# A state space output turned from token-major to channel-major, in a one-core hybrid layer kernel

## The chip, the core and the metric

The kernel runs on one core of a Trainium2 chip. The metric is the device time of one launch in microseconds (us). Beside it there is one profiled execution, from which all rows below are read.

## The reference, cut to what matters

Two layers, each a feed-forward block, a mixer and a second feed-forward block, over 256 tokens of width 1024, all in float32. The change touches the state space half of the mixer:

```python
x = xh * dt[..., None]                                  # 16 heads of 64 channels, 256 tokens
decay = segsum_exp(adt)                                 # per head, 256 x 256, causal
cb = einsum('bclgn,bcsgn->bcgls', cc, bc)               # per group (2 groups of 8 heads)
y = einsum('bcgls,bcgels,bcsgep->bclgep', cb, decay, x) # one chunk of 256: no carried state
...
y = y + xh * d_skip[:, None]
y = y.reshape(bsz, L, D_SSD) * silu(z)
yg = y.reshape(bsz, L, SSD_GROUPS, D_SSD // SSD_GROUPS)
yg = yg * rsqrt(mean(yg * yg, axis=-1) + EPS)           # norm over the 512 channels of a group
return yg.reshape(bsz, L, D_SSD) * norm_g
```

The projection `u = rmsnorm(h) @ w_mix_in` gives z, the convolved channels, dt, q, k, v and the index vectors. The mixer ends with one product of the concatenated state space and attention outputs with `w_mix_out`.

## The kernel before

**Products.** Every large product is done with its operands split into a high and a low part (`whi`/`wlo` for weights, pairs of `tT` tiles for activations), three matmuls for each block of 128 rows. Token-major products (function `three`, lines 182 to 184) hold 128 tokens as the stationary operand and stream 512 weight columns. Channel-major products (lines 866 to 868) hold 128 weight columns and stream all 256 tokens. Small products in plain float32 are one call in the code and two passes in the trace.

**Weights.** `Stream` loads blocks of 2048 columns into `raw` (three buffers), ScalarE makes `whi` (line 127), VectorE makes `wlo` (line 128), three blocks ahead of their use. The DMAs are issued on SyncE's queue.

**Order.** `MIX_ORDER` says in which order the mixer's column blocks are projected. A number is a pair of 128-channel chunks for the convolution, a name is a token-major block: `z0` and `z1` are the two halves of the gate z. Side work is written as generators, `index` (choice of keys), `steps` (decay sums), `ssd` (state space) and `attention`. `flow.step` advances one of them between parts of the projection, `flow.defer` puts a function off by a number of units, `flow.unit` is called after each part. The scheduler then orders each engine's instructions; what is given to `keep_in_program_order` stays behind the instruction traced ahead of it on its engine.

**The state space part.** `conv` (lines 671 to 688) makes each 128-channel chunk `chan[c]`, channels on partitions and tokens along the row. `by_token` turns the chunks into `xs`, tokens on partitions. `ssd` makes, for each group g and for four heads at a time, the matrices `m0` (tokens 0 to 127 against all 256) and `m1` (tokens 128 to 255 against themselves): a DMA broadcasts the decay sums (line 717), ScalarE takes differences and exponentials (lines 719 to 724), VectorE multiplies by dt and cb (lines 727, 729). Then come the products of lines 739 and 743: the matrix is the stationary operand (128 x 128), 64 columns of `xs` stream, 24 such calls in a group. `finish_y` adds x times `d_skip` (GpSimd, line 753; VectorE, line 759), multiplies by silu(z) (line 760), sums squares on ScalarE (`square_sum`, line 427), scales by the row's inverse norm (line 767), and in `turn_y` transposes eight blocks on TensorE (line 774) and splits them into `yT` pairs (`split_scaled`, lines 405 and 407). `yT[0]` to `yT[7]` are read by the mixer's `out_product`.

**PSUM.** Four pools of two banks: `mm` and `ac` for products, `sd` for small products, `tp` for transposes. The state space products hold both `ac` banks.

Of the kernel before, what the change touches and what calls it, by code (L numbers as in the profile page):

```python
# [52 lines left out]
def hybrid_kernel(  # L53
# [39 lines left out]
    def ttile():  # L93
        return tT.tile([P, L], FR, name="tT", tag="tT")
# [98 lines left out]
    for name, c0 in (("z", C_Z), ("q", C_Q), ("k", C_K), ("v", C_V)):  # L193
        for n in range(2):
            MIX_COLS[f"{name}{n}"] = [(c0 + 512 * n, 512)]
    MIX_ORDER = ["idx0", "idx1", 8, "z0", 10, 0, "z1", 2, 4, "q0", 6, "q1", "k0", "k1", "v0", "v1"]
# [106 lines left out]
    heads = const.tile([P, 3, DEPTH, H_SSD], F32, name="heads")  # L303
# [21 lines left out]
    def setup():  # L325
# [4 lines left out]
        with tc.tile_pool(name="setup", bufs=1, reuse_waits="tile") as tmp:  # L330
# [13 lines left out]
            for i, v in enumerate((dt_bias, a_log, d_skip)):  # L344
                later(heads[:, i], v.partition_broadcast(P))
            yield
# [193 lines left out]
    def mixer(l, norm, after):  # L540
        with ExitStack() as mctx:
# [25 lines left out]
            sz, xs = (big8().rearrange("p (t c) -> p t c", t=NT) for _ in range(2))  # L567
# [102 lines left out]

            def conv(c, ps):
                xr = ms.tile([P, L + 3], F32, name="xr", bufs=2)
                nc.gpsimd.memset(xr[:, 0:3], 0.0)
                nc.vector.tensor_mul(xr[:, 3:], ps, rb)

                def w(j):
                    o = (l * 4 + j) * 12 + c
                    return convs[:, o:o + 1]
                o = 96 + l * 12 + c
                acc = row1k()  # L680
                nc.scalar.activation(acc, xr[:, 0:L], AF.Identity, scale=w(0), bias=convs[:, o:o + 1])
                for j in range(1, 4):
                    nc.vector.scalar_tensor_tensor(acc, xr[:, j:j + L], w(j), acc, op0=ALU.mult, op1=ALU.add)
                dst = ms.tile([P, L], F32, name="chan" if c < 8 else "bcs", bufs=4)
                nc.scalar.activation(dst, acc, AF.Silu)
                chan[c] = dst
                if c in (3, 7):
                    flow.defer(lambda: by_token(c // 4), 3)
# [10 lines left out]
            def ssd():  # L699
# [9 lines left out]
                for g in range(G_SSD):  # L709
# [23 lines left out]
                    pss = [bank(ac) for _ in range(NT)]  # L733
                    for t in range(NT):
                        ps = pss[t]
                        for h in range(8):
                            o = ps[:, h * 64:(h + 1) * 64]
                            m0, m1 = ms4[h // 4]
                            nc.tensor.matmul(o, m0[:, h % 4, t * P:(t + 1) * P],  # L739
                                             half[:, 0, h * 64:(h + 1) * 64],  # L740
                                             start=True, stop=(t == 0))
                            if t:
                                nc.tensor.matmul(o, m1[:, h % 4], half[:, 1, h * 64:(h + 1) * 64],
                                                 start=False, stop=True)
# [3 lines left out]
            def finish_y(g, half, pss):  # L748

                sq = [None] * NT  # L750
                for t in range(NT):
                    y = half[:, t].rearrange("p (h c) -> p h c", c=HD_SSD)
                    nc.gpsimd.tensor_tensor(y, y, bc(heads[:, 2, l, 8 * g:8 * g + 8], [P, 8, HD_SSD], 2),
                                            ALU.mult)

                def gate():
                    for t in range(NT):
                        y = half[:, t]
                        nc.vector.tensor_add(y, pss[t], y)
                        nc.vector.tensor_mul(y, y, sz[:, t, 512 * g:512 * g + 512])  # L760
                        sq[t] = square_sum(y, "y")
                    flow.defer(scale)

                def scale():
                    for t in range(NT):
                        rg = inv_rms([sq[t]], D_SSD // G_SSD, "y")
                        nc.vector.tensor_scalar(half[:, t], half[:, t], rg, None, op0=ALU.mult)
                    flow.defer(turn_y)

                def turn_y():  # L770
                    for t in range(NT):
                        ps = bank(tp)
                        for i in range(4):
                            nc.tensor.transpose(ps[:, i * P:(i + 1) * P], half[:, t, i * P:(i + 1) * P], ident)
                        ks = range(4 * g, 4 * g + 4)
                        for k in ks:
                            if yT[k] is None:
                                yT[k] = (ttile(), ttile())
                        split_scaled(ps, [(yT[k], gain(3, l, k)) for k in ks], t)

                flow.defer(gate)


# [74 lines left out]
            for what in MIX_ORDER:  # L858
                if isinstance(what, int):
                    hi, lo = stream.take()  # L860
                    for j in range(2):
# [9 lines left out]
                        flow.unit(0)  # L871
                        conv(what + j, ps)
# [5 lines left out]
                for t, ps in project(norm, n, kind not in "qkv"):  # L878
# [9 lines left out]
                    elif kind == "z":  # L888
                        nc.scalar.activation(sz[:, t, 512 * half:512 * half + 512], ps, AF.Silu, scale=r[t])
# [96 lines left out]
```

## Time and profile before

| | |
|---|---|
| three runs | 1214.01, 1214.35, 1215.32 us; median 1214.35 |
| profiled execution | 1215.21 us, of which its span (first to last instruction) is 1213.5 us |
| TensorE busy | 1198.1 us, 99% of the span, in 5997 instructions |
| VectorE busy | 729.4 us, 60% |
| ScalarE busy | 636.6 us, 52% |
| GpSimd busy | 112.8 us, 9% |
| DMA | 214.25 MB, mean 177 GB/s |

A TensorE instruction's duration in the trace holds its way through the array too, so that instructions overlap: what one costs in a row of like ones is the distance from one start to the next.

### The profile page before, as it was taken

How to read it: one execution, taken by the hardware profiler on the slowest of the kernel's cores; microseconds unless marked ns; L12 is line 12 of the kernel's file. 1: busy time of each engine (PE TensorE's matmuls, PEld its weight loads, DVE VectorE, ACT ScalarE, POOL GpSimd, SP SyncE). 2: the span in 40 equal slices, each digit the busy share in tenths (PEclk: the TensorE clock that was granted, in tenths of full speed). 3: DMA queues.
4: the chain of work that ended last, by engine and by line, in shares of the span. 5: the costliest groups of instructions: out<-in, count | busy, mean ns of one | idle time of the engine just before them, and what ended most of it. 6: DMA issues, size and time to landing. Idle time of an engine off the chain costs nothing.

```text
span 1213.5 us, 15334 instructions
## 1 busy us (share of the span) xinstructions
PE 1198.1 (99%) x5997; PEld 1003.0 (83%) x5997; DVE 729.4 (60%) x963; ACT 636.6 (52%) x864; POOL 112.8 (9%) x216
## 2 busy tenths in 40 slices
PE   8999999999999999999999999999999999999997
PEld 6788888988888888888888888898978888888886
DVE  5655545687597565454464554466867965554543
ACT  5544435657776454444354443366578655444432
POOL 0200000602320000000000000015133100000000
PEclk9999999999999999999999999999999999999999
DMA  7665554654533465564646545566454435556550
GB/s 253 204 202 166 190 190 149 225 174 159 188 140 125 152 202 162 192 206 175 201 151 203 188 163 206 164 200 202 156 174 154 163 135 173 185 165 205 188 193 35
DMA packets 149100, 214.25 MB, mean 177 GB/s; under 512 B 8100, under 2 KB 115364, under 8 KB 149028
## 3 DMA queue, kind: packets, MB, share of 16 engines
q1 hardware_dynamic: 147604, 208.52, 51.9%
q0 software_dynamic: 1280, 4.23, 1.0%
q8 instruction: 47, 0.77, 0.3%
q10 hardware_dynamic: 144, 0.52, 0.1%
q14 instruction: 25, 0.20, 0.1%
HBM read 212.17 MB, written 1.08 MB: 176 GB/s over the span
## 4 chain that ended last, share of the span: by engine, by line
PE 93%; DVE 2%; ACT 2%; DMA 1%; POOL 1%; issue 0%; SPq 0%; ACTq 0%; POOLq 0%; DVEq 0%
PE mm L182 15%; PE mm L184 15%; PE mm L183 15%; PE ac L183 12%; PE ac L184 12%; PE ac L182 12%; PE tp L511 2%; PE ac L739 1%; DMA raw<-in_w_ffn_in_dram 1%; PE mm L866 1%; PE ac L868 1%; PE mm L868 1%; PE ac L867 1%; PE mm L867 1%; PE ac L866 1%; PE sd L800 1%
## 5 line engine op out<-in xcount | busy, mean ns | idle before, releaser
L128 DVE TENSOR_TENSOR wlo<-raw,whi 128x2048 fp32r<-128x2048 f32 (+3 forms) x206 | 451.2, 2195 | 337.5 <-ACT whi L127 337.1
L127 ACT CAST whi<-raw 128x2048 fp32r<-128x2048 f32 (+3 forms) x206 | 376.6, 1835 | 295.7 <-PE ac L184 186.7
L182 PE MATMUL mm<-whi,tT 128*128 128x512 f32 (+1 forms) x672 | 267.6, 398 | 0.5 <-ACT s L894 0.5
L184 PE MATMUL mm<-whi,tT 128*128 128x512 f32 (+1 forms) x672 | 260.8, 388 | 0.4 <-DVE tT L407 0.4
L183 PE MATMUL mm<-wlo,tT 128*128 128x512 f32 (+1 forms) x672 | 260.1, 387 | 0.0
L182 PE MATMUL ac<-whi,tT 128*128 128x512 f32 (+1 forms) x480 | 190.0, 396 | 1.0 <-ACT tT L405 0.5
L183 PE MATMUL ac<-wlo,tT 128*128 128x512 f32 (+1 forms) x480 | 185.1, 386 | 0.8 <-DVE wlo L128 0.8
L184 PE MATMUL ac<-whi,tT 128*128 128x512 f32 (+1 forms) x480 | 185.2, 386 | 0.0
L184 PEld LDWEIGHTS mm<-whi,tT 128*128 128x128 f32 x672 | 126.2, 188 | 26.0 <-DVE tT L407 0.9
L182 PEld LDWEIGHTS mm<-whi,tT 128*128 128x128 f32 x672 | 126.3, 188 | 25.1 <-issue 1.3
L183 PEld LDWEIGHTS mm<-wlo,tT 128*128 128x128 f32 x672 | 126.5, 188 | 22.7 <-DVE wlo L128 0.2
L182 PEld LDWEIGHTS ac<-whi,tT 128*128 128x128 f32 x480 | 90.2, 188 | 17.9 <-ACT whi L127 1.2
L183 PEld LDWEIGHTS ac<-wlo,tT 128*128 128x128 f32 x480 | 90.4, 188 | 17.6 <-DVE wlo L128 1.9
L184 PEld LDWEIGHTS ac<-whi,tT 128*128 128x128 f32 x480 | 90.2, 188 | 17.7
L421 POOL TENSOR_TENSOR r_x<-ms_x,mhalf 128x1 f32<-128x1 f32 x14 | 9.7, 695 | 869.3 <-DVE ms_x L419 861.8
L182 PE MATMUL ac<-whi,hT_hi 128*128 128x512 f32 x176 | 69.2, 393 | 0.0
L182 PE MATMUL mm<-whi,hT_hi 128*128 128x512 f32 x176 | 69.0, 392 | 0.0
L184 PE MATMUL ac<-whi,hT_lo 128*128 128x512 f32 x176 | 68.6, 390 | 0.0
L184 PE MATMUL mm<-whi,hT_lo 128*128 128x512 f32 x176 | 68.6, 390 | 0.0
L183 PE MATMUL mm<-wlo,hT_hi 128*128 128x512 f32 x176 | 68.5, 389 | 0.0
L183 PE MATMUL ac<-wlo,hT_hi 128*128 128x512 f32 x176 | 68.5, 389 | 0.0
L533 ACT ACTIVATE s1k<-ac,r_x 128x256 f32<-128x256 f32 x44 | 20.7, 472 | 67.5 <-PE ac L184 64.7
(217 smaller groups left out, 1449.0 us busy)
## 6 DMA issues: line engine op xcount, KB each, us to landing
raw<-in_w_ffn_in_dram SPq DMA_DIRECT2D x172, 512.0 KB, 5.0
raw<-in_w_ffn_out_dram SPq DMA_DIRECT2D x44, 1024.0 KB, 4.8
raw<-in_w_mix_in_dram SPq DMA_DIRECT2D x44, 1024.0 KB, 5.1
raw<-in_w_mix_out_dram SPq DMA_DIRECT2D x16, 1024.0 KB, 4.8
s<-csum POOLq DMA_DIRECT2D x8, 512.0 KB, 4.0
raw<-in_w_mix_in_dram SPq DMA_DIRECT2D x4, 600.0 KB, 3.8
raw<-in_w_mix_in_dram SPq DMA_DIRECT2D x4, 568.0 KB, 3.9
raw<-in_w_ffn_in_dram SPq DMA_DIRECT2D x8, 256.0 KB, 3.2
```

The source lines that it names most:

```text
L127: pin(nc.scalar.copy(hi[:, o], raw[:, o]))
L128: pin(nc.vector.tensor_sub(lo[:, o], raw[:, o], hi[:, o].bitcast(F32)))
L182: nc.tensor.matmul(ps, xh, whi, start=first, stop=False)
L183: nc.tensor.matmul(ps, xh, wlo, start=False, stop=False)
L184: nc.tensor.matmul(ps, xl, whi, start=False, stop=last)
L511: nc.tensor.transpose(ps[:, f * L + t * P:f * L + (t + 1) * P], hs[:, t, f * P:(f + 1) * P], ident)
L533: nc.scalar.activation(sg, ps[:, 0:256], AF.Silu, scale=norm.r[t])
L739: nc.tensor.matmul(o, m0[:, h % 4, t * P:(t + 1) * P], half[:, 0, h * 64:(h + 1) * 64], start=True, stop=(t == 0))
L800: nc.tensor.matmul(ps[:, j * nk:(j + 1) * nk], qT[:, hg + h0 + j, t * P:(t + 1) * P], kT[:, hg + h0 + j, 0:nk], start=True, stop=True)
L866: nc.tensor.matmul(ps, hi[:, o:o + P], xh, start=(k == 0), stop=False)
L867: nc.tensor.matmul(ps, hi[:, o:o + P], xl, start=False, stop=False)
L868: nc.tensor.matmul(ps, lo[:, o:o + P], xh, start=False, stop=(k == KD - 1))
```

## The change

The z chunks are projected channel-major, as the convolution's chunks are (-8, -6, -4, -2 in `MIX_ORDER` stand for them), and `gate` multiplies by the row of inverse norms (VectorE) and takes silu (ScalarE). The state space products swap operands: 64 columns of `xs` are stationary, `m0` and `m1` stream over 256 and 128 tokens, and two heads write partitions 0 to 63 and 64 to 127 of one bank, that is, use two halves of the array's columns. What follows is done with channels on partitions: skip, gate and squares; the sum over channels by a matmul against a column of ones; the inverse norm brought back as a row by a matmul against the identity; the last scaling and the split into `yT`, without transposes. `d_skip` is laid out by channel with two element-wise DMAs.

```diff
-    MIX_ORDER = ["idx0", "idx1", 8, "z0", 10, 0, "z1", 2, 4, "q0", 6, "q1", "k0", "k1", "v0", "v1"]
+    MIX_ORDER = ["idx0", "idx1", 8, -8, -6, 10, 0, -4, -2, 2, 4, "q0", 6, "q1", "k0", "k1", "v0", "v1"]
...
-            for i, v in enumerate((dt_bias, a_log, d_skip)):
+            for i, v in enumerate((dt_bias, a_log)):
                 later(heads[:, i], v.partition_broadcast(P))
+            for i in range(2):
+                later(skips[64 * i:64 * i + 64], d_skip.rearrange("l (c i) -> i l c", i=2)[i].partition_broadcast(64),
+                      allow_slow_non_contiguous=True)
...
+            def gate(c, ps):
+                nc.vector.tensor_mul(sz[:, c], ps, rb)
+                nc.scalar.activation(sz[:, c], sz[:, c], AF.Silu)
...
-                dst = ms.tile([P, L], F32, name="chan" if c < 8 else "bcs", bufs=4)
+                dst = ms.tile([P, L], F32, name="chan" if c < 8 else "bcs", bufs=8 if c < 8 else 4)
...
-                    pss = [bank(ac) for _ in range(NT)]
-                    for t in range(NT):
-                        ps = pss[t]
-                        for h in range(8):
-                            o = ps[:, h * 64:(h + 1) * 64]
-                            m0, m1 = ms4[h // 4]
-                            nc.tensor.matmul(o, m0[:, h % 4, t * P:(t + 1) * P],
-                                             half[:, 0, h * 64:(h + 1) * 64],
-                                             start=True, stop=(t == 0))
-                            if t:
-                                nc.tensor.matmul(o, m1[:, h % 4], half[:, 1, h * 64:(h + 1) * 64],
-                                                 start=False, stop=True)
+                    pss = [bank(ac) for _ in range(2)]
+                    for h in range(0, 8, 2):
+                        o = pss[h // 4][:, h % 4 * P:h % 4 * P + L]
+                        m0, m1 = ms4[h // 4]
+                        for j in range(2):
+                            tc.keep_in_program_order(
+                                nc.tensor.matmul(o[64 * j:64 * j + 64], half[:, 0, (h + j) * 64:(h + j + 1) * 64],
+                                                 m0[:, (h + j) % 4], start=True, stop=False))
+                        for j in range(2):
+                            tc.keep_in_program_order(
+                                nc.tensor.matmul(o[64 * j:64 * j + 64, P:], half[:, 1, (h + j) * 64:(h + j + 1) * 64],
+                                                 m1[:, (h + j) % 4], start=False, stop=True))
...
+                y = half.rearrange("p b (i t) -> p b i t", i=2)
+
+                def gated():
+                    for b in range(2):
+                        z = sz[:, 4 * g + 2 * b:4 * g + 2 * b + 2]
+                        for i in range(2):
+                            c = 4 * g + 2 * b + i
+                            nc.vector.scalar_tensor_tensor(y[:, b, i], chan[c], skips[:, l, c:c + 1],
+                                                           pss[b][:, i * L:(i + 1) * L],
+                                                           op0=ALU.mult, op1=ALU.add)
+                        nc.vector.tensor_mul(y[:, b], y[:, b], z)
+                        nc.scalar.activation(z, y[:, b], AF.Square)
+                    z = sz[:, 4 * g:4 * g + 4]
+                    nc.vector.tensor_add(z[:, 0:2], z[:, 0:2], z[:, 2:4])
+                    nc.vector.tensor_add(z[:, 0], z[:, 0], z[:, 1])
+                    flow.defer(sums, 2)
+
+                def sums():
+                    ps = bank(sd)
                     for t in range(NT):
+                        nc.tensor.matmul(ps[:, t:t + 1], sz[:, 4 * g, t * P:(t + 1) * P], ones[:, 0:1],
+                                         start=True, stop=True)
+                    m, rg = (small.tile([P, NT], F32, name=n) for n in ("ms_y", "r_y"))
+                    nc.vector.tensor_scalar(m, ps[:, 0:NT], 2.0 / D_SSD, EPS, op0=ALU.mult, op1=ALU.add)
+                    nc.gpsimd.tensor_tensor(rg, m, mhalf.to_broadcast([P, NT]), ALU.pow)
+                    flow.defer(lambda: row(rg))
+
+                def row(rg):
+                    rT = bank(sd)[:, :L]
                     for t in range(NT):
+                        nc.tensor.matmul(rT[:, t * P:(t + 1) * P], rg[:, t:t + 1].to_broadcast([P, P]), ident,
+                                         start=True, stop=True)
+                    scale(rT)
+
+                def scale(rT):
+                    for b in range(2):
+                        for i in range(2):
+                            k = 4 * g + 2 * b + i
+                            hi, lo = ttile(), ttile()
+                            nc.vector.scalar_tensor_tensor(y[:, b, i], y[:, b, i], gain(3, l, k), rT,
+                                                           op0=ALU.mult, op1=ALU.mult)
+                            nc.scalar.copy(hi, y[:, b, i])
+                            nc.vector.tensor_sub(lo, y[:, b, i], hi.bitcast(F32))
+                            yT[k] = (hi, lo)
...
-                        flow.unit(0)
-                        conv(what + j, ps)
+                        flow.unit(what < 0)
+                        if what < 0:
+                            gate(8 + what + j, ps)
+                        else:
+                            conv(what + j, ps)
```

The old bodies of `finish_y` (lines 750 to 781) and the silu of the z blocks (line 889) are taken out.

## Rows read from the trace of the kernel before

**Rows 1.** The page: busy time of the engines, and the granted TensorE clock.
```profile
PE 1198.1 (99%) x5997; PEld 1003.0 (83%) x5997; DVE 729.4 (60%) x963; ACT 636.6 (52%) x864; POOL 112.8 (9%) x216
...
PEclk9999999999999999999999999999999999999999
```
**Rows 2.** Windows, TensorE alone: block z0, then chunk pairs 10 and 0.
```profile
220.91:232.41 11.50, 11.50 (x55) 1.00 0.62 215
232.41:243.93 11.52, 11.52 (x98) 1.00 0.64 189
```
**Rows 3.** Groups by line and shape, TensorE.
```profile
L739 PE MATMUL ac<-s,s 128*128 128x64 f32 x128 | 19.3, 271 | 0.0
...
L743 PE MATMUL ac<-s,s 128*128 128x64 f32 x64 | 12.4, 275 | 0.0
...
L774 PE MATMUL tp<-ident,s 128*128 128x128 f32 x32 | 4.6, 276 | 0.7 <-DVE s L767 0.7
```
**Rows 4.** Timeline of TensorE: transposes, a run of state space products, projection again.
```profile
315.69 0.60 PE L845 MATMUL tp<-ident,s 128*128 128x128 f32 x4
316.12 1.23 PE L739 MATMUL ac<-s,s 128*128 128x64 f32 x10
...
318.52 0.39 PE L743 MATMUL ac<-s,s 128*128 128x64 f32 x2
318.72 0.48 PE L182 MATMUL mm<-whi,tT 128*128 128x512 f32 x1
319.03 0.40 PE L183 MATMUL mm<-wlo,tT 128*128 128x512 f32 x1
```
**Rows 5.** Timeline of TensorE: float32 products over 256 and 128 columns.
```profile
293.08 0.59 PE L704 MATMUL sd<-bcs 128*128 128x256 f32 x2
293.51 0.38 PE L705 MATMUL sd<-bcs 128*128 128x128 f32 x2
293.73 0.60 PE L704 MATMUL sd<-bcs 128*128 128x256 f32 x2
```
**Rows 6.** Timeline of TensorE: index products, 64 rows each, on two halves of the rows.
```profile
302.37 0.39 PE L184 MATMUL mm<-whi,tT 128*128 128x512 f32 x1
302.69 1.14 PE L641 MATMUL sd<-s 64*128 64x256 f32 x8
303.76 0.50 PE L182 MATMUL mm<-whi,tT 128*128 128x512 f32 x1
304.09 0.40 PE L183 MATMUL mm<-wlo,tT 128*128 128x512 f32 x1
```
**Rows 7.** Timeline of TensorE: the last run of state space products in layer 0.
```profile
345.07 0.88 PE L739 MATMUL ac<-s,s 128*128 128x64 f32 x6
```
**Rows 8.** Groups by line and shape, VectorE.
```profile
L407 DVE SCALAR_TENSOR_TENSOR tT<-tp,gains,tT 128x128 fp32r<-128x128 f32 x128 | 36.1, 341 | 14.9 <-ACT tT L405 14.9
L683 DVE SCALAR_TENSOR_TENSOR s1k<-xr,convs,s1k 128x256 f32<-128x256 f32 x72 | 34.6, 485 | 5.9 <-ACT s1k L681 5.1
...
L828 DVE TENSOR_TENSOR tT<-sd,tT 128x256 fp32r<-128x256 f32 x16 | 6.4, 420 | 7.0 <-ACT tT L827 7.0
...
L759 DVE TENSOR_TENSOR s<-ac,s 128x512 f32<-128x512 f32 x8 | 5.4, 676 | 3.9 <-POOL s L753 3.9
...
L767 DVE TENSOR_SCALAR s<-s,r_y 128x512 f32<-128x512 f32 x8 | 3.9, 484 | 2.4 <-POOL r_y L421 2.3
```
**Rows 9.** Windows, all engines: z stretch, then the stretch of the state space products.
```profile
220.90:256.00 35.10, 35.10 (x217) 30.84 (x216) 23.00 (x31) 23.53 (x31) 16.54 (x32) 1.00 0.59 191
320.00:370.00 50.00, 49.44 (x273) 41.91 (x272) 42.09 (x91) 38.43 (x78) 12.88 (x23) 1.00 0.41 139
```
**Rows 10.** Waits of SyncE's queue.
```profile
SPq L114 <- DVE wlo L128: 691.7, 109, 10.2
```
**Rows 11.** The page's DMA queue: packets, MB, share of 16 engines.
```profile
q1 hardware_dynamic: 147604, 208.52, 51.9%
```

More of the change, by code (lines that the diff above doesn't have):

```diff
@@ L192, in hybrid_kernel @@
     }
-    for name, c0 in (("z", C_Z), ("q", C_Q), ("k", C_K), ("v", C_V)):
+    for name, c0 in (("q", C_Q), ("k", C_K), ("v", C_V)):
         for n in range(2):
             MIX_COLS[f"{name}{n}"] = [(c0 + 512 * n, 512)]
-    MIX_ORDER = ["idx0", "idx1", 8, "z0", 10, 0, "z1", 2, 4, "q0", 6, "q1", "k0", "k1", "v0", "v1"]
+    MIX_ORDER = ["idx0", "idx1", 8, -8, -6, 10, 0, -4, -2, 2, 4, "q0", 6, "q1", "k0", "k1", "v0", "v1"]
     X_BEFORE = {0: [(0, 0)], 1: [(1, 0)], 2: [], 4: [(0, 1), (1, 1)], 6: []}
@@ L302, in hybrid_kernel @@
     convs = const.tile([P, 120], F32, name="convs")
-    heads = const.tile([P, 3, DEPTH, H_SSD], F32, name="heads")
+    heads = const.tile([P, 2, DEPTH, H_SSD], F32, name="heads")
+    skips = const.tile([P, DEPTH, H_SSD // 2], F32, name="skips")
     a_neg = const.tile([P, DEPTH, H_SSD], F32, name="a_neg")
@@ L566, in mixer @@
             csum = rowsums.tile([H_SSD, L], F32, name="csum", tag="csum")
-            sz, xs = (big8().rearrange("p (t c) -> p t c", t=NT) for _ in range(2))
+            sz = big8().rearrange("p (c t) -> p c t", c=8)
+            xs = big8().rearrange("p (t c) -> p t c", t=NT)
             kT, qT = (big8().rearrange("p (h c) -> p h c", h=H_ATT) for _ in range(2))
@@ L748, in finish_y @@
             def finish_y(g, half, pss):
[L750 to L756, printed above, removed]
-                    for t in range(NT):
[L758 to L762, printed above, removed]
@@ L764, in scale @@
-                def scale():
-                    for t in range(NT):
[L766 to L779, printed above, removed]
@@ L781, in finish_y @@
-                flow.defer(gate)
+                y = half.rearrange("p b (i t) -> p b i t", i=2)
[13 more added lines that the diff above has]
+                    flow.defer(sums, 2)
@@ L784, in attention @@
+                flow.defer(gated)
             def attention():
@@ L887, in mixer @@
                                                        op0=ALU.mult, op1=ALU.add)
-                    elif kind == "z":
-                        nc.scalar.activation(sz[:, t, 512 * half:512 * half + 512], ps, AF.Silu, scale=r[t])
                     elif kind == "v":
```

## The prediction

> **What bounds the kernel now.** Read the page's busy times first: TensorE is busy in 99% of the span and its granted clock reads 9 (90% or more of full speed) in every slice [rows 1], that is, it stays at the 2.4 GHz level. VectorE stands at 60%, ScalarE at 52%. So the time is the sum of TensorE's starts, and a change is worth what it adds to or takes from that sum, unless another engine starts to hold TensorE up. Next the groups by line, for how many passes each small product has [rows 3]; then the timeline around them, because a group's mean duration (0.27 us) holds the way through the array, while the distance between starts is the cost [rows 4 to 6]; last the windows of the two stretches that change, for the room on the other engines [rows 9].
>
> **The change, step by step.**
>
> *z by channel.* Block z0 takes 11.50 us with five index transposes inside [rows 2]. Four transposes take 0.43 us [rows 4], so the five cost 0.54, with some 0.1 for coming back; 10.9 us are left for 48 passes over 512 columns, 0.227 each. Two chunk pairs, the same weights with weights stationary and 256 columns streaming, take 11.52 us [rows 2]: 96 passes, 0.120 each. So each z block costs 0.6 us more, and there are four: **+2.4 us**. VectorE gets 16 multiplications of 128x256 in each layer, 0.42 us each (as line 828's [rows 8]), 6.7 us in each layer of a region where it is busy 23.0 of 35.1 us [rows 9]; ScalarE takes as many silus in place of eight longer ones. Both fit in, so I cost them at nothing. If they didn't, every us that a bank comes free late would stand on TensorE's path. The weights come in pieces of 1 KB in place of 2 KB, as the chunk pairs' do; the DMA share with them is 0.64, with z0 0.62 [rows 2]: nothing.
>
> *The products of the state space part.* Now 192 passes [rows 3]. A run of 24 (10 and seven pairs) goes from 316.12 to 318.72, 0.108 each [rows 4]: 20.8 us. They stream only 64 columns, so something other than the stream sets this pace. Afterwards there are 64 calls, 128 passes, half over 256 columns, half over 128, each on half of the array's columns. In plain float32 a pass over 256 columns costs 0.215 us and one over 128 costs 0.11 [rows 5]. If the halves do not overlap: 64 x 0.215 + 64 x 0.11 = 20.8 us, no gain. If they overlap fully, half: 10.4 us. No row shows two column halves; the nearest are the index products on two halves of the rows: eight passes over 256 columns take 1.07 us from their first start to the next projection pass [rows 6], where one after the other would be 1.72. I take full overlap, with the entry and the exit costed next: **-10.4 us**; the bounds are -10.4 and 0.
>
> *Changing the array's shape.* From 302.37 to 304.09 are 1.72 us [rows 6]: two projection passes (0.454), four pairs of 0.215 (0.86), and 0.41 left for going in and out. The plain run costs only the longer step after it, 0.31 in place of 0.227 [rows 4], about 0.09. So a run of half-array products costs 0.32 more. There are 7 runs in layer 0, from the one at 316.12 [rows 4] to the one at 345.07 [rows 7]; 14 in all. Afterwards four heads' matrices come at a time, four times in a layer, in one or two runs each: 8 to 16 in both layers, at the extreme 32 (every two heads alone, and those cut once more). I take 12: **+3.8 us**, between 2.6 and 10. The Trainium skill says the same in TensorEngine Tiling (Array Packing), Tiling Modes: changing the tiling mode drains the engine; rows 6 agree, with 0.41 us for a run. TensorE: Matmul & The Clock Gate, Part 3, gives 2.38 times for three column tiles; taken as 1.6 times for two, an estimate from that page, these products would take 13 us, and the sum would come out 1.2 us lower than mine.
>
> *Transposes out, sums and rows in.* 32 transposes of `turn_y` go [rows 3], 0.108 each: -3.5. Added in each of four groups: two calls over one column and two over 128, two passes each, 16 + 16 passes at about 0.11 (the 64-column passes show that few columns do not make a pass cheaper): +3.5. Four small steps in a layer take the place of `turn_y`'s two or three; I count one more excursion in each, 0.09: **+0.2**.
>
> *Waits.* TensorE waited 0.7 us for line 767 ahead of `turn_y` [rows 3]; this goes. In its place the sums wait for VectorE's additions and the row for GpSimd's power; both are put off by a unit or more (some 5 us), so I give them the like, 0.25 for each of four: **+0.3** net, between -0.7 and +3.
>
> *VectorE and GpSimd in that stretch.* In a group `finish_y` had 4 x 0.68, 2 x 0.48 and 8 x 0.34, 6.4 us; now four fused operations on 256 columns (0.49), two products and an addition on 512 (0.68), one on 256 (0.42), four more fused (0.49) and four subtractions (0.42), 8.1 us [rows 8]. That is +1.7 in a group, 3.4 in a layer, where VectorE is busy 42.1 of 50 us [rows 9]: 91% afterwards. I cost it at nothing, with `wlo` made up to three blocks ahead as the cover. GpSimd's skip product goes, for which line 759 waited 3.9 us [rows 8]. The chain to `yT` gets one unit longer, but the second group's pairs are first read three `out_product` steps in.
>
> *d_skip by channel.* Two DMAs of 1024 four-byte pieces on SyncE's queue, ahead of a weight block. At the mean time of a packet, 51.9% of 16 x 1213.5 us over 147604, 0.068 us [rows 11], 2048 pieces hold the 16 engines 8.7 us once. The queue spends 692 us waiting for free buffers [rows 10], so loads run ahead: nothing, at worst some us in layer 0's first block. The larger `chan` pool only takes waits away.
>
> *Sum:* +2.4 - 10.4 + 3.8 + 0.2 + 0.3 = **-3.7 us**. The profiled execution took 1215.21 us, 1.7 more than its span of 1213.5 and 0.9 more than the median of 1214.35; nothing outside the span changes, so the difference goes onto the median: 1210.6 us.
>
> **The rivals.**
>
> *The column halves run one after the other.* For it: rows 6 show row halves alone, where each stream feeds its own 64 rows; two column halves need two streams of 128 rows at once. Against: the array is split there too, and eight passes end in 1.07 us. Then the products cost 0 in place of -10.4: +6.7 with the price of changing shape, +2.9 without it: 1217.3 to 1221, slower.
>
> *VectorE becomes the bound of the state space stretch.* Mechanism: VectorE's 3.4 us more in each layer make `wlo` late, and TensorE waits on line 183. It decides the sign once more than 3.7 us of the 6.8 get through. For it: 91% busy. Against: TensorE's only wait there now is short, and three blocks lie ahead. All of it through: 1217.4 us.
>
> *Loads are not hidden.* Mechanism: two column halves share their rows, so each pair of passes first waits for its weight load, 64 steps of about 0.1 us (the pace of the 64-column passes, [rows 4]): +6.4, 1217 us. Rows 6 speak against it: 1.07 us for four pairs leave 0.2 in all above the streams. In the skill's words (TensorE: Matmul & The Clock Gate, Part 3) a load overlaps passes in flight only when the row group differs; rows 4 show full-array loads keeping a 0.108 pace, so the trace does not bear the rule out.
>
> *More gain.* Runs stay whole and the stretch's stalls go with the shorter chain: going in and out costs 2.6, waits -0.7 and a stall of some 0.5 in each layer goes with them: 1214.35 + 2.4 - 10.4 + 2.6 + 0.2 - 0.7 - 1 = 1207.4 us or somewhat less.
>
> **How the numbers follow.** A measurement of this kernel can tell 0.2%, 2.4 us, from no change: faster ends at 1211.9, slower starts at 1216.8. Forecast 0.56 (its own range 1208 to 1213: 0.43 faster, 0.13 the same). Halves one after the other 0.18 (slower). VectorE 0.10 (part of it through: 0.05 the same, 0.05 slower). Loads 0.06 (0.03 the same, 0.03 slower). More gain 0.10 (faster). In sum: faster 0.53, same 0.21, slower 0.26. The range takes in the gain's tail and most of the three rivals above: 1206 to 1219 leaves out the upper half of the first rival and little else.
>
> **What would show it.** The state space products of the profile after: pairs of starts a few ns apart and a step of 0.215 for each pair over 256 columns if the halves overlap; one start every 0.215 if not. The z chunks in steps of 0.120. The runs counted, and the step around each (0.41). `turn_y` gone from the groups, sums and rows with 0.11 a pass. In the chain of waits no VectorE line above 1 us between 320 and 375. The prediction is wrong if TensorE's starts fall by much more or less than 3.7 us, or if its idle time, now about 1% of the span with the start-up in it, grows in the two mixers.

## The result, and the profile after

The changed kernel takes 1222.58 us (median of four, 1222.39 to 1222.84), the kernel before 1214.55 us (median of four): 1.0062 times as long, with an interval of 1.0049 to 1.0074. Instead of 3.7 us less it takes 8.0 us more. The profiled execution took 1222.39 us, its span is 1220.7 us.

The page of the changed kernel answers to [rows 1] and [rows 11]: busy times, the granted clock, the DMA queue.

```profile
PE 1197.6 (98%) x6125; PEld 1002.7 (82%) x6125; DVE 741.1 (61%) x983; ACT 633.1 (52%) x848; POOL 97.6 (8%) x204
...
PEclk9989999999999999999999999999999999999999
...
q1 hardware_dynamic: 153636, 208.51, 52.1%
```

TensorE's busy time is the same as before within 0.5 us, but the span is 7.2 us longer, and in the third slice (61 to 92 us) the granted clock reads 8 for the first time. That is layer 0's first feed-forward block, a stretch in which the change puts no work on TensorE. TensorE's waits say what for (total, times, longest):

```profile
PE mm L182 <- ACT whi L127: 6.8, 1, 6.8
...
PE mm L183 <- DVE wlo L128: 1.5, 1, 1.5
```

One wait of 6.8 us for a weight's high part, then 1.5 us for its low part. The timeline shows both waits, and what stood behind them:

```profile
61.70 0.39 PE L184 MATMUL mm<-whi,tT 128*128 128x512 f32 x1
66.97 1.90 ACT L127 CAST whi<-raw 128x2048 fp32r<-128x2048 f32 x1 [12.53 <-DMA raw<-in_w_ffn_in_dram]
68.91 2.29 DVE L128 TENSOR_TENSOR wlo<-raw,whi 128x2048 fp32r<-128x2048 f32 x1 [13.73 <-ACT whi L127]
...
68.92 0.79 PE L182 MATMUL mm<-whi,tT 128*128 128x512 f32 x1 [6.84 <-ACT whi L127]
...
71.25 0.79 PE L183 MATMUL mm<-wlo,tT 128*128 128x512 f32 x1 [1.53 <-DVE wlo L128]
...
72.27 0.63 PE L182 MATMUL mm<-whi,tT 128*128 128x512 f32 x1
...
72.70 0.63 PE L183 MATMUL mm<-wlo,tT 128*128 128x512 f32 x1
```

Read it from the back. TensorE's pass is due at 61.93 (0.23 after 61.70) and starts at 68.92: 7.0 us. The next one starts 2.33 later in place of 0.23: 2.1 us. From then on starts are 0.43 us apart, not 0.227, for some four microseconds: the 1.2 GHz level, another 2 us. Together 11 us. ScalarE stood idle for 12.5 us before its cast, because the weight block had not come. Ahead of that block in the DMA queue are the two loads of `skips`. The tile's own view gives their time to landing, and the view of the transfers from 36 to 75 us what was moved (40 slices of 0.975 us: busy tenths of the DMA engines, GB/s):

```profile
L330 SPq DMA_DIRECT2D skips<-in_d_skip_dram x2: 647/706/766, 38.7 to 39.4; - x2
...
DMA to landing us min/median/max: 13.1/18.1/23.1
```

```profile
DMA  0199950000000000000000000279999999830699
GB/s 14 23 270 289 383 145 0 0 0 0 0 0 0 0 0 0 0 0 0 0 0 0 0 0 10 69 238 373 379 358 350 347 348 337 284 126 34 154 301 333
```

For 18 slices, 42 to 59 us, nothing but the four-byte pieces is under way: 0 GB/s, and the engines read as idle too. The second load, issued at 39.4, lands 23.1 us later, at 62.5, and only shortly before that do the weights flow again. The queue's row for the 17 us from 42 to 59 us alone (packets, MB, share of 16 engines):

```profile
q1 hardware_dynamic: 1785, 0.01, 4.6%
```

One piece takes 0.15 us on each of the 16 engines (16 x 17 / 1785), if they share them evenly, but the recorded 4.6% comes to 0.007 us a piece. So a packet's recorded time does not hold what one of these pieces costs; that is why the page's 52.1% looks harmless. The windows show the clock (third column from the right) falling in the stall and returning:

```profile
60.00:65.00 5.00, 2.08 (x10) 1.37 (x8) 0.00 (x0) 0.00 (x0) 0.00 (x0) 1.00 0.77 260
65.00:70.00 5.00, 0.79 (x1) 0.29 (x1) 1.09 (x1) 1.92 (x2) 0.00 (x0) 0.58 1.05 336
70.00:75.00 5.00, 3.75 (x9) 2.98 (x10) 3.88 (x3) 2.25 (x2) 0.00 (x0) 0.50 0.63 191
75.00:80.00 5.00, 5.00 (x23) 3.98 (x22) 1.17 (x2) 1.70 (x3) 0.00 (x0) 0.90 0.81 266
```

The part that the change is about did what was forecast. TensorE's timeline of a run of state space products, which answers to [rows 4]:

```profile
327.79 0.60 PE L870 MATMUL tp<-ident,s 128*128 128x128 f32 x4
328.32 0.65 PE L750 MATMUL ac<-s,s 128*64 128x256 f32 x4
328.80 0.39 PE L754 MATMUL ac<-s,s 128*64 128x128 f32 x4
329.02 0.60 PE L750 MATMUL ac<-s,s 128*64 128x256 f32 x4
329.45 0.39 PE L754 MATMUL ac<-s,s 128*64 128x128 f32 x4
329.77 0.50 PE L182 MATMUL mm<-whi,tT 128*128 128x512 f32 x1
330.11 0.40 PE L183 MATMUL mm<-wlo,tT 128*128 128x512 f32 x1
```

Sixteen passes in 1.45 us. Four passes over 256 columns take 0.43 to 0.48 us from their first start to the next group, where four in a row would be 0.86 [rows 5]: the halves overlap. Comparing where the same transposes of `h_res` start in the two traces tells where the rest went: +11.1 us by the end of the first feed-forward block, then -2.8 in mixer 0, -2.5 in mixer 1, and 0.4 to 0.5 us more in each of the three other feed-forward blocks; in all +7.2. The mixers gained what was forecast, and more; the loss is outside them.

### The profile page after: what moved, and what is told of

Same layout as the page of the kernel before. It is cut to its first block, busy times and chain, and to the rows that moved or that the text cites. A ratio compares the mean times of both kernels' runs of the same rounds, so it can differ in the third digit from the quotient of the medians.

```text
span 1220.7 us, 15579 instructions
## 1 busy us (share of the span) xinstructions
PE 1197.6 (98%) x6125; PEld 1002.7 (82%) x6125; DVE 741.1 (61%) x983; ACT 633.1 (52%) x848; POOL 97.6 (8%) x204
## 3 DMA queue, kind: packets, MB, share of 16 engines
q1 hardware_dynamic: 153636, 208.51, 52.1%
## 4 chain that ended last, share of the span: by engine, by line
PE 89%; DVE 4%; DMA 3%; ACT 2%; issue 1%; POOL 0%; SPq 0%; ACTq 0%; POOLq 0%; DVEq 0%
PE mm L184 13%; PE mm L183 13%; PE mm L182 13%; PE ac L184 11%; PE ac L182 11%; PE ac L183 11%; DMA raw<-in_w_ffn_in_dram 3%; PE mm L891 2%; PE mm L893 2%; PE ac L891 2%; PE mm L892 2%; PE ac L892 2%; PE ac L893 2%; PE tp L516 2%; DVE wlo L128 1%; PE sd L825 1%
## 5 line engine op out<-in xcount | busy, mean ns | idle before, releaser
L182 PE MATMUL mm<-whi,tT 128*128 128x512 f32 (+1 forms) x640 | 256.0, 400 | 6.8 <-ACT whi L127 6.8
L183 PE MATMUL mm<-wlo,tT 128*128 128x512 f32 (+1 forms) x640 | 248.7, 389 | 1.5 <-DVE wlo L128 1.5
L184 PE MATMUL mm<-whi,tT 128*128 128x512 f32 (+1 forms) x640 | 249.1, 389 | 0.2 <-DVE tT L412 0.2
L182 PE MATMUL ac<-whi,tT 128*128 128x512 f32 (+1 forms) x448 | 176.9, 395 | 0.9 <-ACT tT L410 0.6
L183 PE MATMUL ac<-wlo,tT 128*128 128x512 f32 (+1 forms) x448 | 173.2, 387 | 0.8 <-DVE wlo L128 0.8
L184 PE MATMUL ac<-whi,tT 128*128 128x512 f32 (+1 forms) x448 | 172.9, 386 | 0.0
L182 PEld LDWEIGHTS mm<-whi,tT 128*128 128x128 f32 x640 | 120.9, 189 | 30.6 <-ACT whi L127 7.3
L183 PEld LDWEIGHTS mm<-wlo,tT 128*128 128x128 f32 x640 | 121.0, 189 | 25.2 <-DVE wlo L128 3.0
L184 PEld LDWEIGHTS mm<-whi,tT 128*128 128x128 f32 x640 | 120.7, 189 | 25.1 <-DVE tT L412 0.5
L183 PEld LDWEIGHTS ac<-wlo,tT 128*128 128x128 f32 x448 | 84.4, 188 | 16.9 <-DVE wlo L128 1.9
L182 PEld LDWEIGHTS ac<-whi,tT 128*128 128x128 f32 x448 | 84.2, 188 | 16.8 <-ACT whi L127 1.2
L184 PEld LDWEIGHTS ac<-whi,tT 128*128 128x128 f32 x448 | 84.1, 188 | 16.5
L538 ACT ACTIVATE s1k<-mm,r_x 128x256 f32<-128x256 f32 x44 | 20.6, 472 | 68.0 <-PE mm L184 67.4
```

The costliest lines, as they stand in the source:

```text
L182: nc.tensor.matmul(ps, xh, whi, start=first, stop=False)
L183: nc.tensor.matmul(ps, xh, wlo, start=False, stop=False)
L184: nc.tensor.matmul(ps, xl, whi, start=False, stop=last)
L538: nc.scalar.activation(sg, ps[:, 0:256], AF.Silu, scale=norm.r[t])
```

## The experiments

**The load alone taken out.** The first theory: the element-wise load is the whole loss, and without it the change gains its 3.7 us. The rival: the loss lies in the change itself, and the load is only where it shows. `d_skip` is loaded as one contiguous broadcast, as before, and VectorE lays it out by channel.

```diff
-            for i in range(2):
-                later(skips[64 * i:64 * i + 64], d_skip.rearrange("l (c i) -> i l c", i=2)[i].partition_broadcast(64),
-                      allow_slow_non_contiguous=True)
+            dsk = tmp.tile([P, DEPTH, H_SSD], F32, name="dsk")
+            later(dsk, d_skip.partition_broadcast(P))
...
+            for i in range(2):
+                a = slice(64 * i, 64 * i + 64)
+                nc.vector.tensor_copy(skips[a], dsk[a].rearrange("p l (c i) -> p i l c", i=2)[:, i])
```

> Changed kernel, but d_skip comes in as one contiguous broadcast and two VectorE copies lay it out by channel. Theory A (the element-wise d_skip load starves the weight stream of layer 0's first block; the rest of the change gains what TensorE's starts say): the 7 us stall at 62 us is gone, time 1210.5 us, 1209 to 1212, faster than the kernel before. Theory B (the loss lies in the mixers, the stall at the start is an accident of the schedule): at least 1218 us.

Measured: 1211.54 us (six runs, 1211.38 to 1212.29) beside 1215.26 for the kernel before, ratio 0.9969 (0.9958 to 0.9981). The load lands in 5.7 us and the same stretch has no stall and the full clock:

```profile
60.00:65.00 5.00, 5.00 (x24) 4.12 (x24) 4.11 (x3) 2.24 (x2) 0.00 (x0) 1.00 0.46 138
65.00:70.00 5.00, 5.00 (x25) 4.08 (x24) 1.17 (x2) 2.35 (x3) 0.00 (x0) 1.00 0.84 281
70.00:75.00 5.00, 5.00 (x24) 4.10 (x23) 4.03 (x2) 2.79 (x3) 0.00 (x0) 1.00 0.15 42
```

So the load costs 1222.58 - 1211.54 = 11.0 us, as read from the timeline, and the rest of the change gives 3.7 us. (The two differences from the kernel before, 8.0 and 3.7, each taken with its own runs of that kernel, make it 11.7.)

**The load alone put in.** The kernel before with the two element-wise loads, which nobody reads.

```diff
+    skips = const.tile([P, DEPTH, H_SSD // 2], F32, name="skips")
...
+            for i in range(2):
+                later(skips[64 * i:64 * i + 64], d_skip.rearrange("l (c i) -> i l c", i=2)[i].partition_broadcast(64),
+                      allow_slow_non_contiguous=True)
```

> Kernel before, with the two element-wise d_skip loads added at the place where the changed kernel has them; nothing reads what they bring, and all else is the kernel before. Theory A: the same stall of 7 to 9 us on a whi wait near 62 us and the low clock after it, 1225.5 us, 1223 to 1228. Theory B: 1214.5 us.

Measured: 1228.93 us, ratio 1.0115 (1.0101 to 1.0129): 13.7 us, somewhat more than the 11.0 and 0.9 above the range expected. Its waits repeat those above, one more included, and the clock stays low longer:

```profile
PE mm L182 <- ACT whi L127: 7.6, 1, 7.6
...
PE ac L182 <- ACT whi L127: 1.9, 1, 1.9
PE mm L183 <- DVE wlo L128: 1.5, 1, 1.5
```

```profile
70.00:75.00 5.00, 1.03 (x2) 0.52 (x3) 2.29 (x1) 3.39 (x2) 0.00 (x0) 0.50 0.91 289
75.00:80.00 5.00, 5.00 (x15) 3.90 (x16) 2.69 (x2) 1.12 (x3) 0.00 (x0) 0.58 0.82 263
```

Both directions agree, so the load is the cause, with nothing of the state space part needed.

**Half of the load.** The same with one of the two loads (`range(1)`). If the cost were in proportion to the pieces, it would be some 7 us; if the stream's lead is a threshold, next to nothing.

> Kernel before with one of the two element-wise d_skip loads added (1024 pieces, some 10 us of the DMA engines; nothing reads it). If the weight stream's lead of some 10 us is a threshold, as theory A has it: nearly all of it is hidden, 1215 to 1217.5 us, less than half of what both loads cost. If every piece costs its share: half of the 13.7 us, 1222 us.

Measured: 1217.0 us (ten runs), ratio 1.0014 (1.0005 to 1.0024): +1.9 us, as much as the transposes of `h_res` behind the first block start later (206.6 us where it was 204.7). The load lands 14.6 us after its issue. So the cost is not in proportion but has a threshold: 14.6 us of blocked queue cost 1.9, 23.6 us (the later of the two loads in the run with both) cost 13.7.

**The load in four parts.** The changed kernel with four loads of 512 pieces, put ahead of different steps of the set-up.

```diff
+            later(skips[0:64, 0], d_skip.rearrange("l (c i) -> i l c", i=2)[0, 0].partition_broadcast(64),
+                  allow_slow_non_contiguous=True)
...
+            later(skips[64:128, 0], d_skip.rearrange("l (c i) -> i l c", i=2)[1, 0].partition_broadcast(64),
+                  allow_slow_non_contiguous=True)
```

(and the same for the second layer, further on)

> Changed kernel, the element-wise load cut into four of 512 pieces each, some 5 us apart in the set-up. If a weight block is only late by what stands ahead of it (the lead of the stream takes up some 9 us): each part delays one block by 5 us or so, no stall, 1211 us. If the pieces' total time on the DMA engines counts: 1216 to 1222 us.

Measured: 1213.1 us (ten runs), ratio 0.9985 (0.9976 to 0.9994). The transfers from 36 to 75 us show weights moving between the parts:

```profile
DMA  6007998000005995000499610049960002999999
GB/s 153 5 1 173 308 387 239 3 0 0 0 17 188 383 348 140 9 0 5 142 349 368 210 22 0 8 123 370 370 202 5 0 1 61 330 381 368 352 346 306
```

The time lies between the two that were expected, nearer to the first. The same 2048 pieces cost 1.6 us over the load made contiguous, in place of 11.0: what counts is how long the weights stand still at a stretch, not how many pieces there are in all. No single load takes over 12.9 us to land.

**Another queue.** The two loads issued from ScalarE's queue in place of SyncE's. If the weights were held up because they were queued behind the loads, this frees them.

```diff
-                later(skips[64 * i:64 * i + 64], d_skip.rearrange("l (c i) -> i l c", i=2)[i].partition_broadcast(64),
-                      allow_slow_non_contiguous=True)
+                tc.keep_in_program_order(nc.scalar.dma_start(skips[64 * i:64 * i + 64], d_skip.rearrange("l (c i) -> i l c", i=2)[i].partition_broadcast(64),
+                      allow_slow_non_contiguous=True))
```

> Changed kernel, the two element-wise loads issued by ScalarE on its own queue at the same place. If the cost is the order on SyncE's queue, where weight pieces stand behind the small ones: weights overtake them, 1211 us. If it is the time of the pieces on the 16 DMA engines whoever issues them: 1218 to 1223 us.

Measured: 1220.41 us, ratio 1.004 (1.0024 to 1.0055). Only 2.2 us better (2.9 by the two differences from the kernel before); here the two loads are also issued 5 us apart (35.3 and 40.3 us), so even that is not the queue's alone. The transfers from 36 to 75 us, and two rows of SyncE's queue (start, duration of the issuing instruction):

```profile
DMA  2000000000369741000011135799999995028999
GB/s 75 5 0 0 0 0 0 0 0 5 122 214 300 264 150 43 6 6 6 8 20 28 16 92 200 266 343 397 351 351 330 336 303 181 26 45 270 321 384 338
```

```profile
37.40 0.92 SPq L114 DMA_DIRECT2D raw<-in_w_ffn_in_dram  x2
38.37 6.48 SPq L330 DMA_DIRECT2D heads<-in_dt_bias_dram  x1
```

The weights that SyncE issues at 37.4 us do not move until 45 us, and from 52 to 58 us weights slow to between 6 and 28 GB/s; between the two stretches they run at up to 300 GB/s. So the pieces hold up the weights from another queue too. What it is that they hold is not shown. The DMA engines are one candidate; whatever hands them the pieces is another, for an issuing instruction of SyncE takes 6.48 us there, where the same one takes 0.50 us in the changed kernel.

**The column halves taken out.** From the kernel with the contiguous load: two heads' 128 columns stationary, `m0` and `m1` of each head streamed in turn over the whole array. The second head's result overwrites the first's, so the kernel leaves out the output of every first head. This is the rival "one after the other" made real.

```diff
-                                nc.tensor.matmul(o[64 * j:64 * j + 64], half[:, 0, (h + j) * 64:(h + j + 1) * 64],
+                                nc.tensor.matmul(o, half[:, 0, h * 64:(h + 2) * 64],
                                                  m0[:, (h + j) % 4], start=True, stop=False))
...
-                                nc.tensor.matmul(o[64 * j:64 * j + 64, P:], half[:, 1, (h + j) * 64:(h + j + 1) * 64],
+                                nc.tensor.matmul(o[:, P:], half[:, 1, h * 64:(h + 2) * 64],
                                                  m1[:, (h + j) % 4], start=False, stop=True))
```

> As e1_skip_on_chip, but each state space call takes both heads' 128 columns of xs as its stationary operand and writes all 128 rows, so that no two calls share the array; the second head's call overwrites the first's, so the output of every first head is left out. If the overlap of the two column halves is worth what the trace says (128 passes one after the other at 0.215 and 0.11 us, 20.8 us, against 14.3 with the entries and exits): 6 us over e1, 1217.5 us. If the mixers gained by waits and not by the overlap: within 1.5 us of e1.

Measured: 1218.47 us, ratio 1.0028 (1.0017 to 1.004), 6.9 us over the kernel with halves. Its run, to be held beside the one above:

```profile
318.32 0.60 PE L752 MATMUL ac<-s,s 128*128 128x256 f32 x2
318.75 0.38 PE L755 MATMUL ac<-s,s 128*128 128x128 f32 x2
...
320.86 0.47 PE L182 MATMUL mm<-whi,tT 128*128 128x512 f32 x1
```

Sixteen passes take 2.54 us in place of 1.45. The overlap is real and worth 6.9 us, and a kernel without it would have been slower than before.

**The norm in one step.** From the kernel with the contiguous load: a matrix of ones as the stationary operand gives the sum on every partition at once, and GpSimd raises all 128x256 values to the power, so that no row has to be brought back.

```diff
-                    nc.gpsimd.tensor_tensor(rg, m, mhalf.to_broadcast([P, NT]), ALU.pow)
...
+                    nc.tensor.matmul(ps, ones, sz[:, 4 * g], start=True, stop=True)
...
+                    nc.gpsimd.tensor_tensor(rr, rr, mhalf.to_broadcast([P, L]), ALU.pow)
```

> As e1_skip_on_chip, with sums and row in one: ones as a 128x128 stationary operand and the 256 squared tokens streamed give the sum on every partition, then mean and power on 128x256. TensorE: 2 passes of 0.215 us in place of 8 of 0.11 in each of four groups, and one excursion less: 2 us less, 1209.5 us, if GpSimd's power over 256 elements (no row shows its time) comes within the unit that follows; if it is some 5 us or more and holds up GpSimd's rotations of q and k, no gain or a loss of 1 to 3 us.

Measured: 1381.94 us, ratio 1.1373 (1.1356 to 1.139). The expectation fell through on one duration that no row had shown (GpSimd's group, then TensorE's waits):

```profile
L785 POOL TENSOR_TENSOR s1k<-s1k,mhalf 128x256 f32<-128x256 f32 x4 | 166.4, 41604 | 48.4 <-DVE s1k L784 48.4
```

```profile
PE sd L840 <- DVE s L857: 81.4, 2, 40.7
PE mm L182 <- ACT whi L127: 70.8, 2, 35.4
```

The power takes 41.6 us for 256 values a partition, 0.16 us each; in the changed kernel it is 0.72 us for two. Four of them are 166 us; against the kernel with the contiguous load the loss is 1381.94 - 1211.54 = 170.4.

**Addresses.** The kernel with the contiguous load gains in the mixers but gives back some 0.45 us in each feed-forward block, where the change alters no instruction. What does change there is where the buffers lie: `heads` is smaller, `skips` is new. A pad of 64 bytes a partition among the constants puts the buffers behind them where they were, by the sizes in the code (384 bytes of `heads` before, 256 and 64 of `skips` after).

```diff
+    pad = const.tile([P, 16], F32, name="pad")
+    nc.gpsimd.memset(pad, 0.0)
     a_neg = const.tile([P, DEPTH, H_SSD], F32, name="a_neg")
```

> As e1_skip_on_chip, with 64 bytes of padding among the constants, so that every buffer after them lies where it lay in the kernel before. The feed-forward blocks, which the change does not touch, took 0.45 us longer each in the changed kernels, 1.9 us in all. If that is a matter of addresses: the blocks fall back to 176.9 us of matmul starts and the time to 1209.7 us. If not: as e1, 1211.5 us.

Measured: 1210.18 us, ratio 0.9959 (0.9944 to 0.9974). The same kernel once more, on another chip and in more runs:

> The kernel of e8_same_addresses once more, for a firm ratio to the kernel before: 1210 us, 0.9960 (0.995 to 0.997), if the sum of TensorE's starts is right with the load and the addresses taken out.

Measured: 1210.21 us (1209.03 to 1210.78), ratio 0.9956 (0.9942 to 0.997). And with a pad of 32 bytes (`[P, 8]`):

> As e1_skip_on_chip with 32 bytes of padding in place of 64, so that the buffers after the constants start at a multiple of 512 bytes by the sizes in the code. If the matmul starts get shorter the nearer the buffers lie to such a line: feed-forward blocks at or under 176.9 us and 1209 to 1210 us. If only the old place is good: 177.3 us and 1211.5 us.

Measured: 1210.48 us, ratio 0.9962 (0.9949 to 0.9974), between the two that were expected. These intervals overlap with each other and with the unpadded kernel's; the traces tell the kernels apart. The last transposes of `h_res` open the last feed-forward block. The rows of that tile (minimum, median and longest ns, then the first and last start) are, in this order, of the kernel before, of the unpadded one, of the one with 64 bytes and of the one with 32.

```profile
L453 PE MATMUL tp<-ident,h_res x96: 270/272/474, 5.0 to 1026.2; 128*128 128x128 f32 x96
```

```profile
L460 PE MATMUL tp<-ident,h_res x96: 270/272/421, 5.0 to 1022.5; 128*128 128x128 f32 x96
```

```profile
L462 PE MATMUL tp<-ident,h_res x96: 270/272/474, 5.0 to 1021.2; 128*128 128x128 f32 x96
```

```profile
L462 PE MATMUL tp<-ident,h_res x96: 270/272/474, 5.0 to 1021.9; 128*128 128x128 f32 x96
```

From the last start to the end of the span this block takes 187.3 us before (span 1213.5), 187.8 unpadded (1210.3), 187.2 with 64 bytes (1208.4) and 187.5 with 32 (1209.4); the run repeated on another chip gives 187.3 again (1208.5). The second feed-forward block, timed from one group of these transposes to the next, tells it more sharply, for it holds neither the start nor the end of the kernel: 186.95 us before; 187.41 to 187.51 in the five runs with 64 bytes fewer (the changed kernel, the contiguous load, the load in four, the other queue, the whole array); 187.01 and 186.98 with the 64 bytes back, on two chips; 187.15 with half of them. The two runs that put `skips` into the kernel before move the later buffers by 64 bytes the other way: 187.15 both, so some 0.2 us a block of what they lost is this and not the load.

So moving the later buffers back by 64 bytes takes the loss away, half of that takes about half. That the place of the buffers does it is shown, since the pad is the only difference; what in an address matters is not, since a few distances make no rule. Nor is it shown why the block takes 188.72 us in the kernel with the norm in one step, in which small tiles fall away as well.

## Why the prediction was wrong, point by point

**The step that failed: "d_skip by channel ... nothing, at worst some us in layer 0's first block".** The place was right and the price was not. Two numbers behind it failed. First, the "mean time of a packet", 0.068 us: it is a mean over packets of mostly 1 KB and more [rows 11], taken for four-byte pieces, and it counts only time recorded as busy. Measured, 2048 pieces take 23.1 us to land where 8.7 us were forecast; if the 16 engines share them evenly, that is 16 x 23.1 / 2048 = 0.18 us for each with the way to landing in it, or 0.15 by the 17 us in which nothing else moved. Second, "loads run ahead" as a cover without a size. In that block the lead is 12 to 14 us, an estimate (14.6 us blocked, with 1.9 lost; 23.6 blocked, with some 11 of stall). The queue's 692 us of waits [rows 10] are a total over the whole run and say nothing of the lead at one place. The forecast's 8.7 us would have fitted under it; 23.1 do not. The step then missed a consequence: a stall of 7 us takes TensorE to the 1.2 GHz level for some 4 us, 2 us more. None of the signs under "What would show it" looks at that block either.

No row of the prediction shows a load in such pieces, so the term needed an upper bound, and the mean of other packets is none. The trace of before does hold one, the 256 four-byte pieces of `pos_i`, and it would have misled. It lands in 5.0 us, and the 1.5 us from 35.3 to 36.8 us, in which it is moved, hold 432 packets under 512 B, beside weights:

```profile
pos_i<-in_positions_dram SPq DMA_DIRECT2D x1, 1.0 KB, 5.0
```

```profile
DMA packets 600, 0.19 MB, mean 128 GB/s; under 512 B 432, under 2 KB 599, under 8 KB 599
```

That is some 290 in a microsecond, and of `d_skip` 105. So four bytes alone do not make a piece slow. `pos_i` reads each of its values once, each load of `d_skip` reads the same 16 values for 64 partitions; whether that makes the difference, no run tested.

The Trainium skill, DMA: Bandwidth & Descriptors, Specifications, gives 512 B as the least transfer for line rate. The trace agrees: with four-byte pieces alone under way the engines moved 0 GB/s.

**z by channel, +2.4.** Right. The window answers to [rows 2] and lies wholly in z chunks:

```profile
243.02:254.54 11.52, 11.52 (x98) 1.00 0.60 183
```

96 steps of 0.120 us.

**Products, -10.4 with full overlap, and shape changes, +3.8.** Right in sum. All steps of these products come to 14.4 us where they were 21.4, so -7.0; forecast -6.6. The runs are 10, not 12, five in a layer, and one costs about 0.36 us to go in and out instead of 0.41. (Set against the 14 runs of before, the term would have been 12 x 0.41 - 14 x 0.09 = 3.7.) The Trainium skill, TensorEngine Tiling (Array Packing), Tiling Modes, says that a change of tiling mode drains the engine; the trace agrees, with these 0.36 us. From the 2.38 times for three column tiles in the Trainium skill, TensorE: Matmul & The Clock Gate, Part 3, the prediction had estimated 1.6 times for two; here they are as good as twice as fast (0.43 us for four passes, 0.86 in a row).

**Transposes out, sums and rows in, +0.2.** Right: 1.4 and 2.0 us of steps for sums and rows, where `turn_y` had 3.4. The groups:

```profile
L791 PE MATMUL sd<-ident,r_y 128*128 128x128 f32 x16 | 2.6, 287 | 0.2
...
L781 PE MATMUL sd<-ones,s 128*128 128x1 f32 x16 | 2.0, 228 | 0.0
```

**Waits, +0.3.** Too dark: the sums never wait, the row 0.2 us in all, and the 0.7 us of [rows 3] went. One wait is new and was not in the sum, 0.6 us in all of the products (line 750) for VectorE. With the above this makes up most of what the mixers gave beyond the sum: -2.7 and -2.5 us in the kernel with the contiguous load, 5.2 in place of 3.7.

**VectorE at nothing.** Right. In the stretch that answers to [rows 9] it is busy 93% of the time (91% forecast) and TensorE more than 99%:

```profile
331.00:381.00 50.00, 49.62 (x260) 39.71 (x259) 46.69 (x95) 38.85 (x72) 7.91 (x17) 1.00 0.45 161
```

The fused operations took 0.47 us, the products on 512 columns 0.75, near their rows. So `wlo` came in time, and the rival "VectorE becomes the bound" is refuted here, if with little room.

**The other rivals.** "One after the other" is refuted by the timeline, and priced by its experiment: 1218.47, inside the 1217.3 to 1221 worked out, though some 2 us of it is the loss in the feed-forward blocks. Its two mixers take 0.9 and 1.1 us more than before, where the sum without a change of shape said 2.9 in all. "Loads are not hidden" is refuted by the timeline too: 16 passes with 16 weight loads in 1.45 us, 0.36 above the passes for going in and out, no 0.1 us for each load. The rule of the Trainium skill (TensorE: Matmul & The Clock Gate, Part 3) that a load overlaps passes in flight only when the row group differs is not borne out for these column halves, by the same 1.45 us.

**A sum that was right by chance.** The kernel with the contiguous load gains 3.7 us by the medians and 3.2 by the two spans (1213.5 and 1210.3). That is 5.2 gained in the mixers, less the feed-forward blocks' loss to addresses, about 0.5 in each of four, 2.0. No step of the sum had the second term, and the first was 1.5 larger than its terms: that the forecast of 3.7 came out once the load was gone is luck. With the addresses put back the change gives 1215.33 - 1210.21 = 5.1 us (ratio 0.9956), the best version found. The rival "more gain", 1207.4, was not reached: it had the runs fewer and the waits gone, and both came, but smaller.

## What to carry to other kernels

Cost a DMA in small pieces by a measured time to landing of one like it, not by its bytes and not by the queue's mean packet, and hold that time against the lead of the stream it stands in at that place: here a load below the lead cost 1.9 us, one above it 11 to 13.7, the clock included. A small table in another layout is cheaper loaded contiguously and laid out on the chip: two small VectorE copies here in place of 11 us. When a change moves time in blocks that it does not touch, look at what it did to the buffers' addresses before looking for a cause in the code.

## What the runs showed of the hardware that was not expected

- The element-wise load of `d_skip` holds up the weights behind it without reading as busy: in the changed kernel the window from 42 to 60 us reads a DMA share of 0.05 and 0 GB/s while its pieces were under way at 0.15 us each on 16 engines, and weights issued from another queue stood still or slowed to between 6 and 28 GB/s.
- Two column halves with weights of 128 rows each overlap fully in float32: four passes over 256 columns in 0.43 us.
- GpSimd's power costs 0.16 us a value along the row, 41.6 us for 128x256.
- A shift of all later buffers by 64 bytes a partition changes a feed-forward block of 187 us by some 0.5 us, in seven runs alike.
